# Gate and branch products interleaved in a hybrid encoder layer, with four of eight weight pairs as seven products in three gates

## The chip, the cores and the metric

The kernel runs on one core of one Trainium2 chip. The metric is device time in microseconds (us); of several runs of a kernel the median is given. TensorE (PE) multiplies, VectorE (DVE) and ScalarE (ACT) prepare operands and take results out of PSUM, GpSimd (POOL) does a few small things, and SyncE (SP) issues the weight loads.

## What is computed

One encoder layer on 256 tokens of 2048 features. The part around the change is the gated merge of two attention branches:

```python
h = rms_norm(x, norm_mix_pre[l])
proj = jnp.einsum('bsd,dc->bsc', h, w_in[l])
qa, ka, va, qn, kn, vn, gates = jnp.split(proj, split_at, axis=-1)
...
g_a, g_b = jnp.split(jax.nn.sigmoid(gates), N_BRANCHES, axis=-1)
mixed = (g_a * jnp.einsum('bsc,cd->bsd', oa, w_branch_a[l])
         + g_b * jnp.einsum('bsc,cd->bsd', on, w_branch_b[l]))
y = jnp.einsum('bsd,de->bse', mixed, w_out[l])
```

`oa` and `on` (256 x 1024) come from the two attentions. Behind `y` stand a residual, a norm and an MLP (2048 to 8192, squared ReLU, back to 2048) with another norm and residual.

## The kernel before, in words

All products are made in float32 precision from two-part operands: each operand is split into a rounded high part and the rest (`h` and `l` in the tile names), and a product takes three matmuls (high x high, high x low, low x high). A matmul of the wide products has a 128 x 128 stationary piece of the activations and 512 columns of weights.

The two gates and the two branch products are made in two halves of 1024 output columns (`h` = 0 and 1 in the code). Each is a wide group: the weights come in pairs, a pair being 256 rows x 1024 columns, loaded by one DMA of 1 MB. A gate has eight pairs (2048 rows), a branch product four (1024 rows). A group's results stand in PSUM banks named 1, 2, 3 and 7, one for each quarter of 128 tokens x 512 columns; other groups use the same four PSUM buffers in turn. There are two ways to multiply a pair:

- the plain way (`eight`, line 755): 4 quarters x 2 row blocks x 3 matmuls = 24 matmuls. ACT rounds the raw pair to its high part (line 675), DVE subtracts for the low part (line 677).
- seven products of sums (`seven`, line 743), a Winograd form of the 2 x 2 block product: 7 x 3 = 21 matmuls, into banks 1, 2, 3 and also 0, 4, 5 and 6. It needs sums of the weight blocks, so DVE makes three additions (lines 681 to 683), ACT rounds raw blocks (line 680) and sums (line 693), and DVE subtracts for their low parts (lines 684 and 694). It also needs sums of the activations, made once per pair in `h_sums` (line 824) while the first gate runs. Once the last such pair of a group is multiplied, `combine` (line 761) copies bank 0 (ACT, line 767) and makes four additions on DVE (lines 768 to 771), and so puts banks 0, 4, 5 and 6 into the result tiles in SBUF.

At the end of a group each quarter is taken out of its bank. A gate's quarter is added to the result tile if there were seven-product pairs (DVE, line 884) and goes through a sigmoid (ACT, line 885). A branch's quarter is multiplied with the gate (DVE, line 917), and for branch b added to that of branch a (line 919).

The order of the work is that of the code, refined by a scheduler that places every engine's instructions by a modelled timeline. The groups stand in the order ga, gb, ba, bb for each half; the list of weight requests (line 846 on) must have the same order. `Weights.next` keeps three pairs in hand: there are three buffers each for the raw, high and low weights, so a pair's high part waits until the pair three places earlier is multiplied, and its load until that pair is split. Five smaller buffers hold the split sums, of which a seven-product pair takes four. In the very first gate all eight pairs are plain; in the other three the list `MIXED` (line 841) says in which places stand the three seven-product pairs: pairs 0, 3 and 6, in places 1, 3 and 5 of places 0 to 7. While ba of the second half runs, the transposes of the first half's merged result (`mixed_T`, mT in the names) are put between its products. `y` follows bb of the second half.

Of the kernel before, what the change touches and what calls it, by code (L numbers as in the profile page):

```python
# [32 lines left out]
QA, KA, VA, QN, KN, VN, GA, GB = 0, 1024, 2048, 3072, 4096, 5120, 6144, 8192  # L33
# [17 lines left out]
def encoder_layer(ctx: ExitStack, tc: tile.TileContext, a, out):  # L51
# [13 lines left out]
    def page(shape, dt, name):  # L65
        return pages.tile(shape, dt, tag="pg", name=name)
# [4 lines left out]
    def t2k(name, dt=F32):  # L71
        return tmp.tile([P, 2, T], dt, tag="t2k", name=name, bufs=7)
# [128 lines left out]
    def advance(n):  # L201

        if chores:
            with tc.issue_after(last_load[0]):
                chores.pop(0)()
        for _ in range(n):
            if pending:
                g = pending.pop(0)
                if next(g, None):
                    pending.append(g)  # L210
# [507 lines left out]
    def columns(src, i, c):  # L718
        return src[i * T : (i + 1) * T, c : c + 1024].rearrange("(k p) c -> p k c", p=P)
# [53 lines left out]
    def wide_group(name, kinds, weights, stat7, stat8, mm_banks, z, piece, each=None, turn=None, after={}, in_order=False):  # L773

        any7 = any(s for _, s in kinds)
        pr = Products(name, mm_banks)
        pr.in_order = in_order
        for n, (i, seven) in enumerate(kinds):  # L780
            w = weights.next(after)
            if each:
                each(n)
            if seven:
                final = not any(s for _, s in kinds[n + 1 :])
                pr.seven(partial(stat7, i), w, final)
                if final:
                    pr.combine(z)
                continue
            end = n == len(kinds) - 1  # L790
            if turn and n < 2:
                ahead = [*ahead, (i, w)] if n else [(i, w)]
                for t in range(2) if n else ():
                    for ii, ww in ahead:
                        for which in (2 * t, 2 * t + 1):
                            pr.eight(partial(stat8, ii), ww, which, False)
                    if not t:
                        turn()
                continue
            for which in range(4):  # L800
                pr.eight(partial(stat8, i), w, which, end)
                if end:
                    b, t, half = PLAIN[which]
                    piece(t, half, pr.ps[b], any7)

    def sums_of(p1, p2, name):

        a11, a21, a12, a22 = p1[:, :P], p1[:, P:], p2[:, :P], p2[:, P:]
        s = page([P, 4, P], F32, f"{name}s")
        nc.vector.tensor_sub(s[:, 0], a21, a22)  # L810
        nc.vector.tensor_sub(s[:, 1], a11, a21)
        nc.vector.tensor_sub(s[:, 2], s[:, 0], a11)
        nc.vector.tensor_add(s[:, 3], a12, s[:, 2])
        parts_ = page([P, 2, 4, P], F32R, name)
        nc.scalar.copy(parts_[:, 0], s)
        nc.vector.tensor_sub(parts_[:, 1], s, parts_[:, 0].bitcast(F32))
        return parts_
# [5 lines left out]
    def h_sums(i):  # L823
        f = t2k(f"hf{i}")
        for k in range(2):
            d = hT[i][:, k].bitcast(F32)
            nc.vector.tensor_add(f[:, k], d[:, :T], d[:, T:])
        hsum[i] = sums_of(f[:, 0], f[:, 1], f"hs{i}")
# [9 lines left out]
        d = oT[o, i * 2 + k]  # L838
        return d[:, t * P : (t + 1) * P], d[:, T + t * P : T + (t + 1) * P]

    MIXED = [(1, 0), (0, 1), (2, 0), (3, 1), (4, 0), (6, 1), (5, 0), (7, 0)]
    ALL8 = [(i, 0) for i in range(8)]
    mT = []
    mixed = []
# [1 line left out]
    for h in range(2):  # L846
        for nm, src, c, kinds in (
            ("ga", w_in, GA, MIXED if h else ALL8),
            ("gb", w_in, GB, MIXED),
            ("ba", a["w_branch_a"], 0, ALL8[:4]),  # L850
            ("bb", a["w_branch_b"], 0, ALL8[:4]),
        ):
            for i, seven in kinds:
                gw.ask(columns(src, i, c + h * 1024), f"{nm}{h}_{i}", seven)
    gw.stop = 8

    def mixed_T(h, n):

        mh, ml = page([P, 4, T], F32R, f"mh{h}{n}"), page([P, 4, T], F32R, f"ml{h}{n}")
        for b in range(2):  # L860
            pt = bank(f"mT{h}{n}{b}")
            for j in range(2):
                for t in range(2):
                    c = (n * 4 + b * 2 + j) * P
                    nc.tensor.transpose(
                        pt[:, j * T + t * P : j * T + (t + 1) * P],
                        mixed[h][t].rearrange("p a b -> p (a b)")[:, c : c + P],
                        ident,
                    )
            at = slice(b * 2, b * 2 + 2)  # L870
            src = pt.rearrange("p (j q) -> p j q", j=2)
            nc.scalar.copy(mh[:, at], src)
            nc.vector.tensor_sub(ml[:, at], src, mh[:, at].bitcast(F32))
        mT.append((mh, ml))

    for h in range(2):
        gate = []
        for br, gc in (("a", GA), ("b", GB)):
            z = [page([P, 2, 512], F32, f"g{br}{h}{t}") for t in range(2)]

            def gate_piece(t, half, ps, summed, z=z):
                zt = z[t][:, half]
                if summed:
                    nc.vector.tensor_add(zt, zt, ps)
                nc.scalar.activation(
                    zt, zt if summed else ps, AF.Sigmoid, scale=rx[:, t : t + 1]
                )

            first_one = h == 0 and br == "a"

            def each(n):
                advance(2)
                if n >= 4 and n < 7:
                    h_sums((0, 3, 6)[n - 4])

            wide_group(
                f"g{br}{h}",
                ALL8 if first_one else MIXED,
                gw,
                hstat7,  # L900
                hstat8,
                (1, 2, 3, 7),
                z,
                gate_piece,
                each=each if first_one else None,
            )
            if first_one:
                advance(99)
                temps.close()
                mid = ctx.enter_context(tc.tile_pool(name="mid", bufs=5, reuse_waits="tile"))  # L910
                gw.stop = None
            gate.append(z)
        for br, src, o, z in (("a", a["w_branch_a"], "a", gate[0]), ("b", a["w_branch_b"], "n", gate[1])):

            def br_piece(t, half, ps, summed, z=z, br=br, gate=gate):
                zt = z[t][:, half]
                nc.vector.tensor_mul(zt, zt, ps)
                if br == "b":
                    nc.vector.tensor_add(gate[0][t][:, half], gate[0][t][:, half], zt)

            wide_group(
                f"b{br}{h}",
                ALL8[:4],
                gw,
                None,
                partial(ostat8, o),
                (1, 2, 3, 7),
                None,
                br_piece,
                each=(lambda n: mixed_T(0, n // 2) if n in (0, 2) else None) if h and br == "a" else None,  # L930
            )
        mixed.append(gate[0])
# [239 lines left out]
    for g in range(DFF // 1024):  # L1172
        z = Late(lambda g=g: [page([P, 2, 512], F32, f"u{g}{t}") for t in range(2)])
# [256 lines left out]
```

## Time and profile before

| | us |
|---|---|
| three runs | 1342.76, 1343.35, 1343.53 |
| median | 1343.35 |
| span of the profiled execution, first to last instruction | 1342.7 |
| PE busy in it | 1331.8 |
| DVE busy in it | 1060.9 |
| ACT busy in it | 727.8 |

The profiled execution is given by its span only; the three runs lie 0.06 to 0.83 us above that span. The profile's busy time of PE counts a matmul until its modelled end, so consecutive matmuls overlap in it: a single matmul of 512 columns shows as 0.39 us, and the next one begins earlier than that. For how long PE works on something, the spacing of the starts is read, as the chain of waits gives it.

### The profile page before, as it was taken

The numbers are of one execution on the slowest core, as the hardware profiler recorded it, in microseconds if no ns is written. First come the engines' busy times: TensorE is split into PE (matmuls) and PEld (weight loads), VectorE is DVE, ScalarE is ACT, GpSimd is POOL, SyncE is SP. The second block draws the span as 40 slices with busy tenths as digits, with TensorE's granted clock in tenths as the row PEclk, the third lists the DMA queues.
The fourth block names the chain that finished last, engine by engine and source line by source line (L and its number), as shares of the span: only waits on it lengthen the run. The fifth ranks groups of instructions, "written<-read, shape, count | busy, mean of one in ns | idle before, by whom it ended". The sixth has DMA issues, their size and how long they took to land.

```text
span 1342.7 us, 16224 instructions
## 1 busy us (share of the span) xinstructions
PE 1331.8 (99%) x6315; PEld 1116.9 (83%) x6315; DVE 1060.9 (79%) x1224; ACT 727.8 (54%) x857; POOL 38.5 (3%) x71
## 2 busy tenths in 40 slices
PE   9999999999999999999999999999999999999997
PEld 8888888888888888888888888888888888888885
DVE  7968866677857886655778999999888888898886
ACT  6655554545644454344476665666655555555542
POOL 0000000000000000000100000000000000000000
PEclk9999999999999999999999999999999999999999
DMA  9874755564556655586657677877797998798995
GB/s 347 264 216 164 203 162 183 179 190 157 188 188 208 215 202 184 181 291 193 220 188 265 239 246 277 289 244 246 251 360 289 400 374 318 273 367 335 353 354 202
DMA packets 116028, 335.85 MB, mean 250 GB/s; under 512 B 16752, under 2 KB 17008, under 8 KB 115952
## 3 DMA queue, kind: packets, MB, share of 16 engines
q1 hardware_dynamic: 96560, 266.13, 58.2%
q10 hardware_dynamic: 12672, 43.00, 8.5%
q0 software_dynamic: 6720, 25.69, 4.9%
q8 instruction: 49, 0.80, 0.2%
q14 instruction: 27, 0.22, 0.0%
HBM read 307.01 MB, written 29.61 MB: 251 GB/s over the span
## 4 chain that ended last, share of the span: by engine, by line
PE 98%; DVE 1%; DMA 0%; ACT 0%; DVEq 0%; issue 0%; POOLq 0%; POOL 0%; ACTq 0%
PE u L740 25%; PE p L740 24%; PE ga L740 6%; PE gb L740 6%; PE ba L740 3%; PE bb L740 3%; PE qa_p L221 2%; PE ka_p L221 2%; PE qn_p L221 2%; PE kn_p L221 2%; PE y_p L266 2%; PE y_p L265 2%; PE y_p L264 2%; PE qa_p L223 1%; PE qn_p L223 1%; PE ka_p L223 1%
## 5 line engine op out<-in xcount | busy, mean ns | idle before, releaser
L145 DVE TENSOR_TENSOR y_l<-y_w,y_h 128x1024 fp32r<-128x1024 f32 x32 | 37.9, 1222 | 30.9 <-ACT y_h L137 30.9
L137 ACT CAST y_h<-y_w 128x1024 fp32r<-128x1024 f32 x32 | 32.0, 1051 | 40.9 <-PE y_p L266 32.5
L264 PE MATMUL y_p<-y_h,mh 128*128 128x512 f32 x128 | 50.1, 391 | 0.0
L265 PE MATMUL y_p<-y_l,mh 128*128 128x512 f32 x128 | 49.9, 390 | 0.0
L266 PE MATMUL y_p<-y_h,ml 128*128 128x512 f32 x128 | 49.8, 390 | 0.0
L221 PE MATMUL qn_p<-hT,qn_h 128*128 128x512 f32 x128 | 45.8, 399 | 0.0
L221 PE MATMUL qa_p<-hT,qa_h 128*128 128x512 f32 x128 | 45.1, 413 | 0.5 <-DVE hT L305 0.5
L221 PE MATMUL kn_p<-hT,kn_h 128*128 128x512 f32 x128 | 45.3, 397 | 0.0
L221 PE MATMUL ka_p<-hT,ka_h 128*128 128x512 f32 x128 | 45.1, 398 | 0.0
L740 PE MATMUL u<-u_2h,h2T 128*128 128x512 f32 x128 | 44.0, 396 | 0.0
L740 PE MATMUL u<-u_1h,h2T 128*128 128x512 f32 x128 | 43.4, 390 | 0.0
L740 PE MATMUL u<-u_4h,h2T 128*128 128x512 f32 x128 | 43.2, 391 | 0.0
L740 PE MATMUL u<-u_7h,h2T 128*128 128x512 f32 x128 | 41.0, 389 | 0.0
L740 PE MATMUL u<-u_6h,h2T 128*128 128x512 f32 x128 | 41.0, 389 | 0.0
L223 PE MATMUL qn_p<-hT,qn_l 128*128 128x256 f32 x128 | 35.9, 281 | 0.0
L223 PE MATMUL kn_p<-hT,kn_l 128*128 128x256 f32 x128 | 35.7, 280 | 0.0
L223 PE MATMUL ka_p<-hT,ka_l 128*128 128x256 f32 x128 | 35.2, 282 | 0.0
L223 PE MATMUL qa_p<-hT,qa_l 128*128 128x256 f32 x128 | 32.8, 285 | 0.0
L221 PEld LDWEIGHTS qa_p<-hT,qa_h 128*128 128x128 f32 x128 | 24.5, 197 | 5.5 <-ACT qa_h L143 0.8
L221 PEld LDWEIGHTS qn_p<-hT,qn_h 128*128 128x128 f32 x128 | 24.0, 188 | 5.2
L221 PEld LDWEIGHTS kn_p<-hT,kn_h 128*128 128x128 f32 x128 | 23.9, 188 | 5.2
L221 PEld LDWEIGHTS ka_p<-hT,ka_h 128*128 128x128 f32 x128 | 23.9, 188 | 5.2
(1431 smaller groups left out, 4406.8 us busy)
## 6 DMA issues: line engine op xcount, KB each, us to landing
y_w<-in_w_out SPq DMA_DIRECT2D x16, 1024.0 KB, 5.3
bh<-keeph ACTq DMA_DIRECT2D x30, 512.0 KB, 9.6
bl<-keepl ACTq DMA_DIRECT2D x30, 512.0 KB, 11.0
keeph<-ah POOLq DMA_DIRECT2D x18, 512.0 KB, 3.6
keepl<-al POOLq DMA_DIRECT2D x18, 512.0 KB, 7.8
va_w<-in_w_in SPq DMA_DIRECT2D x8, 1024.0 KB, 5.3
qn_w<-in_w_in SPq DMA_DIRECT2D x8, 1024.0 KB, 5.1
kn_w<-in_w_in SPq DMA_DIRECT2D x8, 1024.0 KB, 5.2
```

Of the source, the lines that this page charges most:

```text
L137: nc.scalar.copy(hi[part], src)
L145: sub = nc.vector.tensor_sub(lo[part], src, hi[part].bitcast(F32)).ins
L221: nc.tensor.matmul(ps[b], hi[:, k % 4, cs], mv, start=(k == 0), stop=False)
L223: nc.tensor.matmul(ps[b][:, :T], lo[:, k % 4, cs], mv[:, :T], start=False, stop=(k == nk - 1))
L264: nc.tensor.matmul(ps[t], sh, hi[:, k % 4], start=(k == 0), stop=False)
L265: nc.tensor.matmul(ps[t], sh, lo[:, k % 4], start=False, stop=False)
L266: nc.tensor.matmul(ps[t], sl, hi[:, k % 4], start=False, stop=(k == nk - 1))
L740: ins = nc.tensor.matmul(self.ps[i], st, mv[:, blk], start=i not in self.begun, stop=last and n == 2).ins
```

## The change

In each half the branch product now follows its own gate: ga, ba, gb, bb. The weight requests follow the same order. `MIXED` has four seven-product pairs instead of three: pairs 0, 2, 4 and 6, in places 0, 2, 4 and 6 (the first, third, fifth and seventh), and the activation sums are made for those four pairs. The very first gate keeps eight plain pairs.

```diff
-    MIXED = [(1, 0), (0, 1), (2, 0), (3, 1), (4, 0), (6, 1), (5, 0), (7, 0)]
+    SUMMED = (0, 2, 4, 6)
+    MIXED = [(0, 1), (1, 0), (2, 1), (3, 0), (4, 1), (5, 0), (6, 1), (7, 0)]
...
             ("ga", w_in, GA, MIXED if h else ALL8),
+            ("ba", a["w_branch_a"], 0, ALL8[:4]),
             ("gb", w_in, GB, MIXED),
-            ("ba", a["w_branch_a"], 0, ALL8[:4]),
             ("bb", a["w_branch_b"], 0, ALL8[:4]),
...
-        for br, gc in (("a", GA), ("b", GB)):
+        for br, gc, src, o in (("a", GA, a["w_branch_a"], "a"), ("b", GB, a["w_branch_b"], "n")):
...
-                if n >= 4 and n < 7:
-                    h_sums((0, 3, 6)[n - 4])
+                if n >= 4:
+                    h_sums(SUMMED[n - 4])
...
-        for br, src, o, z in (("a", a["w_branch_a"], "a", gate[0]), ("b", a["w_branch_b"], "n", gate[1])):
```

Two places show what moves. In the rows a result bank is written as gate or branch, half, bank (gb11 is gate b, half 1, bank 1; the same letters with a small bank number are the result tiles), and a weight tile as group, half, pair and part (gb1_4h is the high part of pair 4; eh0 and el0 are the parts of its sums). A number behind the last underscore counts tiles.

On PE, pair 4 of gate b in the second half. Before, its first rows, all into the plain banks:

```order
L740 MATMUL gb11_4204<-gb1_4h_4278,hT4_129 128x512
L740 MATMUL gb11_4204<-gb1_4l_4279,hT4_129 128x512
L740 MATMUL gb11_4204<-gb1_4h_4278,hT4_129 128x512 x2
L740 MATMUL gb11_4204<-gb1_4l_4279,hT4_129 128x512
L740 MATMUL gb11_4204<-gb1_4h_4278,hT4_129 128x512
L740 MATMUL gb12_4211<-gb1_4h_4278,hT4_129 128x512
L740 MATMUL gb12_4211<-gb1_4l_4279,hT4_129 128x512
L740 MATMUL gb12_4211<-gb1_4h_4278,hT4_129 128x512 x2
```

In the changed program the same pair, from its tenth matmul to its last:

```order
L740 MATMUL gb14_4420<-gb1_4eh0_4478,hs4_3266 128x512
L740 MATMUL gb14_4420<-gb1_4el0_4479,hs4_3266 128x512
L740 MATMUL gb14_4420<-gb1_4eh0_4478,hs4_3266 128x512
L740 MATMUL gb16_4424<-gb1_4eh0_4478,hs4_3266 128x512
L740 MATMUL gb16_4424<-gb1_4el0_4479,hs4_3266 128x512
L740 MATMUL gb16_4424<-gb1_4eh0_4478,hs4_3266 128x512
L740 MATMUL gb15_4428<-gb1_4eh1_4482,hs4_3266 128x512
L740 MATMUL gb15_4428<-gb1_4el1_4483,hs4_3266 128x512
L740 MATMUL gb15_4428<-gb1_4eh1_4482,hs4_3266 128x512
L740 MATMUL gb13_4432<-gb1_4eh1_4482,hT4_129 128x512
L740 MATMUL gb13_4432<-gb1_4el1_4483,hT4_129 128x512
L740 MATMUL gb13_4432<-gb1_4eh1_4482,hT4_129 128x512
```

Pair 4 has become seven products of three matmuls, with the sums hs4 as stationary operand. Over the whole program the order holds 6,304 matmuls and transposes before and 6,295 now; behind the last product of bb, PE's order is the same in both.

On DVE, the end of the same gate. Before, from the last weight subtraction of the gate to the third of the next group (ba):

```order
L677 TENSOR_TENSOR gb1_7l_4379<-gb1_7r_4376,gb1_7h_4378 128x2048
L768 TENSOR_TENSOR gb10_4196<-gb10_4196,gb15_4269 128x512
L677 TENSOR_TENSOR ba1_0l_4411<-ba1_0r_4408,ba1_0h_4410 128x2048
L769 TENSOR_TENSOR gb11_4197<-gb10_4196,gb16_4265 128x512
L770 TENSOR_TENSOR gb10_4196<-gb14_4261,gb10_4196 128x512
L771 TENSOR_TENSOR gb11_4197<-gb14_4261,gb11_4197 128x512
L884 TENSOR_TENSOR gb10_4196<-gb10_4196,gb11_4204 128x512
L677 TENSOR_TENSOR ba1_1l_4441<-ba1_1r_4438,ba1_1h_4440 128x2048
L884 TENSOR_TENSOR gb10_4196<-gb10_4196,gb12_4211 128x512
L884 TENSOR_TENSOR gb11_4197<-gb11_4197,gb13_4218 128x512
L884 TENSOR_TENSOR gb11_4197<-gb11_4197,gb17_4225 128x512
L677 TENSOR_TENSOR ba1_2l_4479<-ba1_2r_4476,ba1_2h_4478 128x2048
```

In the changed program (line 884 is now 885, and the next group is bb):

```order
L677 TENSOR_TENSOR gb1_7l_4580<-gb1_7r_4577,gb1_7h_4579 128x2048
L694 TENSOR_TENSOR gb1_6el1_4553<-gb1_6t1_4542,gb1_6eh1_4552 128x1024
L677 TENSOR_TENSOR bb1_0l_4610<-bb1_0r_4607,bb1_0h_4609 128x2048
L768 TENSOR_TENSOR gb10_4387<-gb10_4387,gb15_4428 128x512
L677 TENSOR_TENSOR bb1_1l_4642<-bb1_1r_4639,bb1_1h_4641 128x2048
L769 TENSOR_TENSOR gb11_4388<-gb10_4387,gb16_4424 128x512
L885 TENSOR_TENSOR gb10_4387<-gb10_4387,gb11_4412 128x512
L770 TENSOR_TENSOR gb10_4387<-gb14_4420,gb10_4387 128x512
L771 TENSOR_TENSOR gb11_4388<-gb14_4420,gb11_4388 128x512
L885 TENSOR_TENSOR gb10_4387<-gb10_4387,gb12_4408 128x512
L885 TENSOR_TENSOR gb11_4388<-gb11_4388,gb13_4432 128x512
L885 TENSOR_TENSOR gb11_4388<-gb11_4388,gb17_4460 128x512
```

The last seven-product pair now stands in place 6, with one plain pair behind it instead of two. So the four additions of `combine` stand among the four that empty the gate's banks, and two weight subtractions of the next group stand ahead of the first of these.

## The prediction

> **What bounds the kernel now.** I read the page first: the busy times, the clock, and the chain that ended last.
>
> ```profile
> span 1342.7 us, 16224 instructions
> ...
> PE 1331.8 (99%) x6315; PEld 1116.9 (83%) x6315; DVE 1060.9 (79%) x1224; ACT 727.8 (54%) x857; POOL 38.5 (3%) x71
> ...
> PEclk9999999999999999999999999999999999999999
> ...
> PE 98%; DVE 1%; DMA 0%; ACT 0%; DVEq 0%; issue 0%; POOLq 0%; POOL 0%; ACTq 0%
> ```
>
> PE is on 98% of the chain, at full clock in every slice. A busy PE alone would prove little, since ends of matmuls are modelled; so I asked for PE's own waits.
>
> ```profile
> PE idle L171 <- POOL ones L163: 1.0, 1, 1.0
> PE qa_p L221 <- DVE hT L305: 0.5, 1, 0.5
> ```
>
> That is the whole list: two waits, both before the first product. From there to the tail PE never waits for an operand or a bank. So a matmul taken out shortens the span by its spacing, and nothing else can shorten it; and whatever makes PE wait lengthens it in full. The spacing is read in the chain in order of time (start, length, what), here the groups from gate b of the first half to ba of the second:
>
> ```profile
> 348.98 41.48 PE gb L740 x183
> 390.46 21.76 PE ba L740 x96
> 412.22 21.76 PE bb L740 x96
> 433.98 41.48 PE ga L740 x183
> 475.46 41.48 PE gb L740 x183
> 516.94 0.87 PE mT L865 x8
> 517.82 10.90 PE ba L740 x48
> ```
>
> Each group begins where the last one ends. A gate has 183 matmuls, which is 5 plain pairs of 24 and 3 of 21, in 41.48 us: 0.2267 us each. A branch has 96 in 21.76: the same 0.2267. So a plain pair is 5.44 us of PE and a seven-product pair 4.76.
>
> **The change part by part.** *Matmuls.* In each of three gates a plain pair becomes a seven-product pair: 3 x 3 = 9 matmuls fewer, 9 x 0.2267 = 2.04 us less. The two orders of PE differ by these 9. [...]
>
> *What the added pairs cost DVE and ACT.* The rows of DVE by shape, from gate b of the second half (busy, mean ns):
>
> ```profile
> L694 DVE TENSOR_TENSOR gb_6el<-gb_6t,gb_6eh 128x1024 fp32r<-128x1024 f32 x2 | 2.4, 1224 | 0.0
> L677 DVE TENSOR_TENSOR gb_5l<-gb_5r,gb_5h 128x2048 fp32r<-128x2048 f32 x1 | 2.3, 2284 | 0.0
> ...
> L684 DVE TENSOR_TENSOR gb_6l<-gb_6r,gb_6h 128x1536 fp32r<-128x1536 f32 x1 | 1.8, 1759 | 0.7 <-ACT gb_6h L680 0.7
> ...
> L681 DVE TENSOR_TENSOR gb_6t<-gb_6r 128x1024 f32<-128x1024 f32 x1 | 1.2, 1226 | 0.0
> ...
> L683 DVE TENSOR_TENSOR gb_6t<-gb_6t,gb_6r 128x512 f32<-128x512 f32 x1 | 0.7, 686 | 0.0
> L682 DVE TENSOR_TENSOR gb_6t<-gb_6t,gb_6r 128x512 f32<-128x512 f32 x1 | 0.7, 685 | 0.0
> ```
>
> A seven-product pair takes 1.23 + 0.69 + 0.69 + 1.76 + 2 x 1.22 = 6.81 us, a plain one 2.28: 4.53 us more in each of three gates. [...] Is there room? The windows of ba in the first half and of the two gates of the second (PE, PEld, DVE, ACT):
>
> ```profile
> 390.50:412.20 21.70, 21.70 (x97) 17.97 (x96) 11.59 (x9) 8.93 (x7) 0.00 (x0) 1.00 0.58 194
> 434.00:475.50 41.50, 41.50 (x184) 34.35 (x184) 36.19 (x34) 22.17 (x17) 0.00 (x0) 1.00 0.60 203
> 475.50:517.00 41.50, 41.50 (x186) 34.33 (x184) 32.45 (x30) 21.07 (x17) 0.00 (x0) 1.00 0.61 203
> ```
>
> With 4.53 more, DVE would have 40.7 or 37.0 us to do in a gate that lasts 41.48 - 0.68 = 40.8. Gate a of the second half is the brimful one, since the multiplications and additions of the branch before it end in its window. I counted it anew for the new order: pairs 2, 4 and 6 at 6.81, pairs 3, 5 and 7 and the next group's first two at 2.28, `combine`, the gate's four adds and the branch's eight operations at 0.68 come to 20.4 + 11.4 + 10.9 = 42.7 us of durations. In a row of DVE's work the next operation starts 0.08 before the last one's recorded end (2.29 long, 2.21 to the next start, in the rows of the gate's end below), so these 39 operations take 3.1 us less: 39.6 of 40.8. It fits, with 1.2 us over. The other two gates stand behind a branch a, which has four such operations, not eight, and behind every gate now comes a branch, where DVE works 11.59 of 21.7 us. The first pair of a gate, now a seven-product one, is prepared in the branch's last places. ACT, at 22.17 of 41.5, takes about 2 us more and has the room. So I put these costs at nothing, under the cover of PE's work; what they cost if the cover is thin is the lead of a pair over its use. For the third seven-product pair of gate b:
>
> ```profile
> L684 DVE TENSOR_TENSOR gb_6l<-gb_6r,gb_6h x1: 1759/1759/1759, 494.1 to 494.1; 128x1536 fp32r<-128x1536 f32 x1
> L740 PEld LDWEIGHTS gb<-gb_6l,hs x1: 188/188/188, 501.1 to 501.1; 128*128 128x128 f32 x1
> ```
>
> DVE is done at 495.9, PE takes it up at 501.1: 5.2 us ahead, after three such pairs in places 1, 3 and 5. If the whole 4.53 us came off this lead, 0.7 would be left.
>
> *The end of a gate.* Here the cover gets thinner: after the last seven-product pair stands one plain pair, not two, so 5.44 us less of PE's work hides `combine`. The next group's first matmul into bank 1 waits until the gate's bank 1 has been added. The DVE rows of before at that place:
>
> ```profile
> 503.32 2.29 DVE L677 TENSOR_TENSOR gb_7l<-gb_7r,gb_7h 128x2048 fp32r<-128x2048 f32 x1 [4.16 <-ACT gb_7h L675]
> 505.53 0.68 DVE L768 TENSOR_TENSOR gb<-gb,gb 128x512 f32<-128x512 f32 x1
> 506.13 2.28 DVE L677 TENSOR_TENSOR ba_0l<-ba_0r,ba_0h 128x2048 fp32r<-128x2048 f32 x1
> 508.33 0.68 DVE L769 TENSOR_TENSOR gb<-gb,gb 128x512 f32<-128x512 f32 x1
> ...
> 512.89 0.69 DVE L884 TENSOR_TENSOR gb<-gb,gb 128x512 f32<-128x512 f32 x1 [2.56 <-PE gb L740]
> 513.50 2.29 DVE L677 TENSOR_TENSOR ba_1l<-ba_1r,ba_1h 128x2048 fp32r<-128x2048 f32 x1
> ```
>
> There bank 1 was added by 513.6, and the gate ended at 516.9: 3.3 us to spare, and the add had itself waited 2.56 us for PE. Now the sum for the new order, from t = 0 at PE's first product of pair 6. The buffer for the next group's first high part comes free about then. Its rounding on ACT takes as long as this one:
>
> ```profile
> 503.86 1.92 ACT L675 CAST ba_0h<-ba_0r 128x2048 fp32r<-128x2048 f32 x1
> ```
>
> so about 2.1. Then DVE: bb_0l to 4.3 (2.2 from start to start); L768, which needs the 18th product of the pair, at 18 x 0.2267 + 0.16 = 4.24, so to 4.9 (0.60 from start to start); bb_1l to 7.1; L769 to 7.7; the add of bank 1 to 8.4. The gate ends at 45 x 0.2267 = 10.2. Margin 1.8 us. Bank 2's add follows L770 and L771 and ends at 10.2, and is needed 12 products into the next group, at 12.9. Nothing waits, if DVE is not more than 1.8 us late.
>
> *The first gate's end.* Its results now go to ba at once. ACT had there the rounding of an activation sum, a table load and four sigmoids:
>
> ```profile
> 340.00 0.62 ACT L815 CAST hs<-hs6s 128x512 fp32r<-128x512 f32 x1
> ...
> 345.12 1.28 ACT L885 ACT_TABLE_LOAD   x1
> 346.41 1.93 ACT L885 ACTIVATE ga<-ga,rx 128x512 f32<-128x512 f32 x3
> ```
>
> Bank 1 was free at 347.1, 1.9 us before 348.98. The fourth activation sum puts one more such rounding, 0.6 us, ahead of it; 1.3 are left. The first reader of the sums is gate b, now 21.76 us later.
>
> *What is moved.* The 16 transposes in ba of the second half are the same 16. The loads are the same 24 pairs a half, in the new order, on SP's queue; gpost, x and w_out follow as before. Behind bb PE's order is unchanged; DVE and ACT swap a few neighbours in the down products, by at most one subtraction of 2.28 us, where the lead is:
>
> ```profile
> L740 PE MATMUL p<-d0100el,bh x4: 389/389/389, 1130.1 to 1132.1; 128*128 128x512 f32 x4
> L694 DVE TENSOR_TENSOR d0100el<-d0100t,d0100eh x2: 1218/1220/1221, 1124.3 to 1125.5; 128x1024 fp32r<-128x1024 f32 x2
> ```
>
> The second subtraction ends at 1126.7, and PE takes it up from 1130.1: 3.4 us. That is nothing either.
>
> **The sum.** 1342.70 - 2.04 = 1340.66 us for the span. The median of the runs lies 0.65 above the span, so 1343.35 - 2.04 = 1341.31 us, 0.15% faster. A measurement of this kernel can tell about 0.2%, 2.69 us, from no change; this is less.
>
> **The rivals.** *Part of the gain goes into waits.* The margins of 1.3 to 1.8 us are sums of steps that each wait for another engine. If DVE comes late by one more subtraction, 2.2 us, at each of three gate ends, PE waits 3 x 0.4 = 1.2 us, and the time is 1342.5. Against it: before, DVE had idle time there. Chance 0.15; the time then lies between 1341.5 and 1345.
>
> *DVE becomes the bound (slower).* The place is the end of a gate. If the whole 4.53 us per gate pile up there, as the window's 40.7 of 40.8 us would have it, the add of bank 1 comes 4.53 - 1.8 = 2.7 us late, and PE waits 3 x 2.7 = 8.2 us: 1341.3 + 8.2 = 1349.5. It turns slower than before once the wait is over 0.68 us per gate, that is DVE over 2.5 us late. Against it: the branch behind every gate, the 1.2 us that even the fullest gate has over, and the 5.2 us lead. Chance 0.06.
>
> *More comes back than nine matmuls.* With no wait of PE's to remove, only the scatter of runs (0.77 us from lowest to highest) can bring 1340.66, the bound for faster. Chance 0.10.
>
> That the change does not do what it says is ruled out by the two orders.
>
> **How the numbers follow.** The forecast, 2.04 us less with all else hidden, has 0.69; read within the scatter it is "no change". Faster by over 0.2% gets 0.10, from the scatter. Slower by over 0.2% (1346.0) gets 0.06, DVE's pile-up. Within 0.2% lie the forecast and the partial waits: 0.69 + 0.15 = 0.84. The range begins at 1341.3 - 0.8 = 1340.5, the scatter, and goes up to 1344.0, a wait of 0.9 us at each of three gate ends.
>
> **What would show it.** In the profile after: three gates of 180 matmuls in 40.80 us each; no wait of PE in the list besides the first two; the add of bank 1 (L885) done 1 to 2 us before the next group's first product. A wait of PE on L885 or L886, or on a low part (L677, L684, L694), would say which margin failed. The prediction is wrong if the spacing is no longer 0.2267, or if the span loses more than 2.04 us.

## The result, and the profile after

| | median, us | lowest to highest | runs |
|---|---|---|---|
| before | 1343.47 | 1342.76 to 1344.45 | 21 |
| after | 1341.61 | 1341.05 to 1342.25 | 21 |

The ratio is 0.9986, 95% interval 0.9980 to 0.9992: 1.86 us less, where 2.04 was forecast. That is less than 0.2%, so "within 0.2%" is what happened, 0.3 us above the forecast of 1341.3 and inside the range.

The page of the changed kernel has the same picture as before: PE busy for nearly the whole span.

```profile
span 1339.9 us, 16240 instructions
...
PE 1328.2 (99%) x6306; PEld 1112.9 (83%) x6306; DVE 1076.7 (80%) x1246; ACT 732.3 (55%) x864; POOL 38.5 (3%) x71
```

DVE has 22 instructions more and is busy for 15.8 us more. PE's own waits (line waited for, us in total, times, longest):

```profile
PE idle L171 <- POOL ones L163: 1.0, 1, 1.0
PE qa_p L221 <- DVE hT L305: 0.7, 2, 0.5
PE qa_p L223 <- DVE qa_l L145: 0.3, 1, 0.3
PE ka_p L221 <- DVE rope_s L291: 0.3, 1, 0.3
```

Two lines are new, but both belong to the projections at the start, over 300 us ahead of anything that the change touches. No gate and no branch is in the list. The chain of waits in order of time shows the groups (start, length, what):

```profile
348.20 21.76 PE ba L740 x96
369.96 40.80 PE gb L740 x180
...
432.97 40.35 PE ga L740 x178
...
496.93 40.80 PE gb L740 x180
537.73 21.76 PE bb L740 x96
559.49 0.23 PE y_p L264
```

A gate has 180 matmuls in 40.80 us (gate a of the second half shows 178, because two of its matmuls were drawn ahead among those of bb). The spacing is still 0.2267 us. From the end of the first gate, 348.20, to the first product of `y`, 559.49, pass 211.29 us. Before, gate b began at 348.98 and bb of the second half ended at 540.48 + 21.76 = 562.24: 213.26 us. The difference is 1.97 us, nine spacings less 0.07 that ba with its transposes takes longer.

The span fell by more, 2.8 us. The missing 0.8 us lies ahead of the first gate's end, which stands at 348.98 in the one profile and at 348.20 in the other. The two differ from PE's first real matmuls on; here the row of before and, in the second fence, the row of after (start, length, and what was waited for):

```profile
5.73 2.05 PE L221 MATMUL qa_p<-hT,qa_h 128*128 128x512 f32 x4 [0.53 <-DVE hT L305]
```

```profile
5.14 1.17 PE L221 MATMUL qa_p<-hT,qa_h 128*128 128x512 f32 x4 [0.51 <-DVE hT L305]
```

The same four matmuls took 2.05 and 1.17 us and end 1.5 us apart (7.78 against 6.31); by the first gate's end 0.8 us of that are left. What slowed them was not tried. In the eleven profiles of this case PE does the same 1,878 matmuls and transposes in the same order up to there, and the first gate ends anywhere from 347.29 to 348.98 us, in the four with the old order of groups from 347.39 to 348.98. So it is taken as scatter of the start, and not as a gain of the change.

### The profile page after: what moved, and what is told of

It reads as the page before. It is cut to its first block, busy times and chain, and to the rows that moved or that the text cites. A ratio compares the mean times of both kernels' runs of the same rounds, so it can differ in the third digit from the quotient of the medians.

```text
span 1339.9 us, 16240 instructions
## 1 busy us (share of the span) xinstructions
PE 1328.2 (99%) x6306; PEld 1112.9 (83%) x6306; DVE 1076.7 (80%) x1246; ACT 732.3 (55%) x864; POOL 38.5 (3%) x71
## 4 chain that ended last, share of the span: by engine, by line
PE 96%; DMA 1%; DVE 1%; ACT 0%; SPq 0%; issue 0%; DVEq 0%; POOLq 0%; POOL 0%; ACTq 0%
PE u L740 25%; PE p L740 24%; PE ga L740 6%; PE gb L740 6%; PE ba L740 3%; PE bb L740 3%; PE qn_p L221 2%; PE kn_p L221 2%; PE y_p L266 2%; PE y_p L265 2%; PE y_p L264 2%; PE ka_p L221 2%; PE qn_p L223 1%; PE kn_p L223 1%; PE qa_p L221 1%; PE vn_p L264 1%
## 5 line engine op out<-in xcount | busy, mean ns | idle before, releaser
L740 PEld LDWEIGHTS u<-u_1h,h2T 128*128 128x128 f32 x128 | 24.0, 188 | 5.0
```

Of the source, the lines that this page charges most:

```text
L740: ins = nc.tensor.matmul(self.ps[i], st, mv[:, blk], start=i not in self.begun, stop=last and n == 2).ins
```

## The experiments

The theory: a matmul taken out of the gates is worth its spacing, and DVE's larger share is hidden; the margin of that cover stands at the end of a gate, on the add of bank 1. The rivals: the new order of the groups has a part in the gain; the cover is larger, or stands elsewhere. All times are medians. In each experiment the loss of PE is read in the trace from the first gate's end to the first product of `y`, which leaves out the scatter of the start. (In the kernel as printed, `seven`, `eight` and `combine` begin at lines 746, 758 and 764, and `h_sums` at line 823.)

**The order alone.** Three seven-product pairs as before, in the new order:

```diff
-    SUMMED = (0, 2, 4, 6)
-    MIXED = [(0, 1), (1, 0), (2, 1), (3, 0), (4, 1), (5, 0), (6, 1), (7, 0)]
+    SUMMED = (0, 3, 6)
+    MIXED = [(1, 0), (0, 1), (2, 0), (3, 1), (4, 0), (6, 1), (5, 0), (7, 0)]
...
-                if n >= 4:
+                if n >= 4 and n < 7:
```

> The new order of groups (each branch behind its gate) with the three seven-product pairs of before, in places 1, 3 and 5: 6,304 matmuls and transposes, as before. Theory (the gain is the nine matmuls and nothing else): three gates of 183 matmuls in 41.48 us each, no wait of PE behind the first product, from the first gate's end to y's first product 213.3 us as before, and the time of before, 1343.5 us, to within 0.4. Rival (the order itself gives a part, by waits or by a closer sequence of groups): the stretch from the first gate's end to y is shorter than 213.0 and the time nearer to 1342.5 or below.

Measured: 1343.00 us beside 1343.23 for before, ratio 0.9999 (0.9990 to 1.0008). The chain of this kernel:

```profile
347.29 21.76 PE ba L740 x96
369.05 41.48 PE gb L740 x183
...
538.80 21.76 PE bb L740 x96
```

From 347.29 to 560.56 it is 213.27 us, as before (213.26). The order by itself moves nothing; the rival falls.

**No seven-product pair at all.** All eight pairs of every gate plain, in the new order (`MIXED` is the list of `ALL8`, `SUMMED` is empty, and no activation sum is made).

> All four gates with eight plain pairs, new order, no activation sums and no final additions: 6,295 + 36 matmuls. It measures the price of a matmul by the time itself, beyond the scatter of the runs. Theory (a matmul left out is worth its spacing of 0.2267 us): 36 x 0.2267 = 8.16 us over the changed kernel, 1349.8 us, gates of 192 matmuls in 43.53 us. [...] Rival (the DVE and ACT work that goes with the seven-product pairs delays something, so that they are worth less than their matmuls): under 7.5 us over, below 1349.1.

Measured: 1349.74 us, 8.13 over the changed kernel. The chain:

```profile
348.09 21.76 PE ba L740 x96
369.85 43.52 PE gb L740 x192
...
545.72 21.76 PE bb L740 x96
```

Here the question is only the size of a matmul, with 36 of them instead of nine, so that the scatter matters little. The time gives 8.13 / 36 = 0.226 us each; the gates give 43.52 / 192 = 0.2267; and from 348.09 to 545.72 + 21.76 = 567.48 it is 219.39 us, 8.10 more than in the changed kernel. So the rival, that the work on DVE and ACT takes something back, falls. The median of before moved by 0.24 us from one series of runs to the next, which over 36 matmuls leaves the price of one open by 0.007 us in the time alone; the spacing in the chain gives it directly.

**The four pairs alone.** Four seven-product pairs in the old order ga, gb, ba, bb (the lines for `SUMMED`, `MIXED` and `h_sums` of the change, nothing else of it).

> Four seven-product pairs in places 0, 2, 4 and 6 in the old order ga, gb, ba, bb: the nine matmuls are gone, but gate b follows gate a at once. Theory (DVE's margins are thin and the branch behind each gate is the cover): gate a's end and gate b's start collide on DVE; PE waits somewhat under 1 us at the start of gate b, for a high part of one of its first pairs, so of 2.04 us some 1.2 to 1.4 are left: about 1342.2 us. Rival 1 (the cover is not needed): no wait of PE, three gates in 40.80 us, 1341.5 us. Rival 2 (DVE becomes the bound when two seven-product gates follow each other): several microseconds of waits on DVE's results in gate b, over 1345 us.

Measured: 1341.24 us, ratio 0.9986 (0.9977 to 0.9995), the same ratio as the whole change. The chain of waits, and below it, from DVE's row of work, the add of bank 1 at the end of gate a of the second half:

```profile
347.39 40.80 PE gb L740 x180
...
431.71 40.80 PE ga L740 x180
472.51 40.83 PE gb L740 x180
...
536.94 21.76 PE bb L740 x96
```

```profile
471.36 0.68 DVE L885 TENSOR_TENSOR ga<-ga,ga 128x512 f32<-128x512 f32 x1
```

From 347.39 to 558.70 it is 211.31 us. No gate waits. My theory of this run, that gate b right behind gate a costs some 0.8 us, falls: on DVE the end of gate a and the start of gate b do run into each other, with work for gate b (lines 681, 682 and 684) between the adds of gate a, but PE loses nothing by it. The add ends at 472.04 and gate b begins at 472.51; these 0.5 us are not a margin, though, as the next experiment shows that gate b's first products do not wait for that add. So with four pairs the cover of the branch is not needed. What it is worth shows only when DVE gets more work.

**One subtraction more at the gate ends, in both orders.** DVE makes one low part of the next group twice, and the add of bank 1 stands behind that:

```diff
+    again = [None]
...
                 nc.vector.tensor_sub(l1, raw, h1.bitcast(F32))
+            if name in ("ba1_1", "bb0_1", "bb1_1"):
+                for _ in range(1):
+                    again[0] = nc.vector.tensor_sub(l1, raw, h1.bitcast(F32)).ins
...
-                    nc.vector.tensor_add(zt, zt, ps)
+                    with tc.issue_after(again[0]) if (t, half) == (0, 1) else nullcontext():
+                        nc.vector.tensor_add(zt, zt, ps)
```

In the old order the names are `ba0_1`, `gb1_1` and `ba1_1`. Line 885 becomes 891.

> The changed kernel with one more 2.2 us subtraction on DVE at each of the three gate ends (the low part of the next branch's second pair is made twice), and the add of bank 1 ordered behind it. Without it that add ends 1.9 us before the next group's first product in front of both bb, and 12 transposes (1.3 us) more lie ahead of ba. Theory (bank 1's add is what the next group waits for, and its margin is 1.9 us): PE waits 0.3 us on L891 at each bb and not at ba; a wait of 0.29 us cost 0.55 us of the sequence with five pairs, so 1.1 us over the changed kernel, about 1342.7. Rival (the margin is larger, or the add is not what is waited for): no wait, 1341.6.

> Four pairs in the old order ga, gb, ba, bb, with one more 2.2 us subtraction and the add of bank 1 behind it at the three gate ends. Without it that add ends 0.5 us before gate b of the second half and 1.5 us before ba of the first half; ahead of ba of the second half stand transposes. Theory (the branch behind each gate is cover that four pairs do not use up, but more DVE work does): waits of 1.7 us and 0.7 us, 0.25 more lost behind each, so 2.9 us over the four pairs in the old order (about 1344.1), against 1.1 in the new one. Rival (the order makes no difference to the cover): the same loss as in the new order, 1.1 us or none.

In the new order: 1342.81 us, 1.20 over the changed kernel. DVE at the end of gate b, second half, and PE at the same place:

```profile
535.64 2.29 DVE L682 TENSOR_TENSOR bb_1l<-bb_1r,bb_1h 128x2048 fp32r<-128x2048 f32 x1
537.84 0.68 DVE L891 TENSOR_TENSOR gb<-gb,gb 128x512 f32<-128x512 f32 x1
```

```profile
537.82 0.39 PE L745 MATMUL gb<-gb_7h,hT 128*128 128x512 f32 x1
538.67 0.47 PE L745 MATMUL bb<-bb_0h,onT 128*128 128x512 f32 x1 [0.46 <-DVE gb L891]
538.98 0.39 PE L745 MATMUL bb<-bb_0l,onT 128*128 128x512 f32 x1
```

PE waits for L891 at both bb and not at ba, as the theory said. Each costs 0.62 + 0.08 = 0.70 us of the sequence (0.85 and 0.31 from start to start instead of 0.2267), 1.4 together. From the first gate's end to `y` PE loses 1.5 us. In the old order: 1344.27 us, 3.03 over the four pairs alone (expected 2.9), and 3.0 us lost by PE in the same stretch. PE's waits in it:

```profile
PE ba L745 <- DVE gb L891: 0.7, 1, 0.7
...
PE gb L745 <- DVE ga L891: 0.5, 1, 0.5
PE gb L745 <- DVE gb_2el L699: 0.4, 1, 0.4
PE gb L745 <- ACT gb_2h L685: 0.3, 1, 0.3
```

At ba of the first half the theory is right: a wait of 0.7 us on the add of bank 1, 1.0 us lost with what follows. At gate b of the second half its 1.7 us on that add did not come. Gate b's first three matmuls began at 473.52 while the add of bank 1 ended only at 475.41, so they do not wait for it; PE lost 2.05 us there in three smaller waits, on the high part of pair 2, on a low part of its sums, and on the second of the gate's adds. That the total came out at the expected 2.9 is luck in this half.

The same edit costs 1.2 us by the medians (1.5 by the stretch) in the new order and 3.0 in the old; beside each other the two kernels differ by 1344.27 - 1342.81 = 1.5 us. Here the rival "the order makes no difference to the cover" falls.

**Two subtractions more.** The same in the new order with `range(2)`.

> As with one repeat, but two of them at each gate end; the add of bank 1 then also stands behind the other additions of the gate's end. Theory: at bb it ends at 14.0 us after the first product of the last seven-product pair where 10.2 are there, so a wait of about 3.9 us at each bb and of about 2.6 at ba, with 0.25 more lost behind each: 11 us over the changed kernel, about 1352.6. Rival (DVE makes up for it, since it has idle time in the gate): under 4 us over, below 1345.6.

Measured: 1355.71 us, 14.1 over the changed kernel instead of 11. The profile is of the longest of the four runs, 1357.86 us. The waits in the list are the ones expected, in their places: 7.7 us in two on L891 at bb, 2.0 at ba. What came on top stands behind them (PE at the end of gate b, first half):

```profile
410.01 0.39 PE L745 MATMUL gb<-gb_7h,hT 128*128 128x512 f32 x1
414.26 0.76 PE L745 MATMUL bb<-bb_0h,onT 128*128 128x512 f32 x1 [3.86 <-DVE gb L891]
414.82 0.63 PE L745 MATMUL bb<-bb_0l,onT 128*128 128x512 f32 x1
415.25 1.05 PE L745 MATMUL bb<-bb_0h,onT 128*128 128x512 f32 x2
416.10 0.63 PE L745 MATMUL bb<-bb_0l,onT 128*128 128x512 f32 x1
```

The starts are 0.43 us apart, not 0.23, up to 419.94. The windows of the same stretch (busy time of PE, PEld, DVE, ACT and POOL, then the granted clock, the share of TensorE's full clock that it was given):

```profile
405.00:411.00 6.00, 5.40 (x24) 4.13 (x22) 6.00 (x6) 0.56 (x1) 0.00 (x0) 1.00 0.52 175
411.00:414.20 3.20, 0.00 (x0) 0.00 (x0) 3.20 (x4) 1.38 (x2) 0.00 (x0) 0.87 0.00 0
414.20:420.00 5.80, 5.74 (x14) 4.51 (x15) 5.06 (x5) 2.51 (x4) 0.00 (x0) 0.50 0.70 199
```

The clock falls to 0.50 toward the end of the wait and stays there to the end of the window. In the profiled execution the three waits themselves cost 4.0 + 2.3 + 4.0 = 10.3 us of PE's sequence from start to start (2.3 at ba and not 2.6, as all 16 transposes stood ahead of it, not 12), and the slow matmuls behind them 2.9 + 1.8 + 1.7 = 6.4. From the first gate's end to `y` PE loses 16.5 us in all. So the theory's sum for the waits is about right, and the rest is a loss that it did not have.

**The same wait, with PE kept busy.** Sixteen matmuls into a spare bank fill the wait at both bb; nobody reads them.

```diff
+                if self.name in ("gb0", "gb1"):
+                    lasts[0] = ins
...
+            if name in ("bb0", "bb1") and n == 0:
+                spare = bank(f"spare{name}")
+                st = stat8(i, 0, 0)[0]
+                dead = lasts[0]
+                for _ in range(16):
+                    with tc.issue_after(dead):
+                        dead = nc.tensor.matmul(spare, st, w[0][:, 1], start=True, stop=True).ins
+                pr.after = dead
```

`lasts[0]` is the gate's last matmul, and `pr.after` puts the group's first product behind the sixteen.

> As two repeats at each gate end, but PE spends the wait at both bb on 16 matmuls whose results nobody reads (16 x 0.2267 = 3.6 of the 4.0 us between the gate's last matmul and the add of bank 1). Two repeats came to 1355.7 us and a span of 1356.1 instead of the expected 1352.6, and behind both waits of 3.9 us matmuls stood 0.43 us apart for some 3 to 6 us at a granted clock of 0.50. Theory (the idle time of PE itself takes the clock down): the first products of both bb stand at the same places behind the gates, but 0.2267 apart and at clock 1.00; of the 6.0 us lost behind the three waits the 4.3 at both bb go, the 1.7 at ba stay, so a span of 1351.8 and a time of 1351 to 1352.6. Rival (the slow matmuls come from what else runs then: loads, ACT and DVE at work behind the gate's end): they stay, and the time too, 1355 to 1357.

Measured: 1352.64 us (expected 1351 to 1352.6), span 1351.3 (expected 1351.8). PE at the end of gate b, first half, and the windows:

```profile
409.74 0.39 PE L746 MATMUL gb<-gb_7h,hT 128*128 128x512 f32 x1
409.96 3.79 PE L796 MATMUL sparebb<-bb_0h,onT 128*128 128x512 f32 x16
413.89 0.50 PE L746 MATMUL bb<-bb_0h,onT 128*128 128x512 f32 x1
414.23 0.40 PE L746 MATMUL bb<-bb_0l,onT 128*128 128x512 f32 x1
```

```profile
413.80:420.00 6.20, 6.11 (x27) 5.04 (x28) 5.55 (x7) 2.86 (x5) 0.00 (x0) 1.00 0.67 198
```

The first product of bb still comes 4.15 us after the gate's last (4.25 without the filling), with DVE and the loads at work as before, but the 6.2 us behind it hold 27 matmuls at clock 1.00, where the 5.8 us without the filling held 14 at 0.50. The wait of 2.0 us at ba was not filled, and the slow matmuls behind it stayed (1.75 us lost). So in these two runs the half clock at bb came with PE's own idle time of 3.9 us and went with it, and the rival falls.

**Five pairs.** A fifth seven-product pair, pair 5, in the three gates:

```diff
-    SUMMED = (0, 2, 4, 6)
+    SUMMED = (0, 2, 4, 5, 6)
-    MIXED = [(0, 1), (1, 0), (2, 1), (3, 0), (4, 1), (5, 0), (6, 1), (7, 0)]
+    MIXED = [(0, 1), (1, 0), (2, 1), (3, 0), (4, 1), (5, 1), (6, 1), (7, 0)]
...
-                if n >= 4:
-                    h_sums(SUMMED[n - 4])
+                if n >= 3:
+                    h_sums(SUMMED[n - 3])
```

> A fifth seven-product pair, pair 5 in place 5, in each of the three gates, new order: 6,286 matmuls and transposes. If DVE still had room, another 9 x 0.2267 = 2.04 us less than with four pairs: 1339.6 us. Theory (in the fullest gate DVE has only about 1 us over with four pairs, and a fifth adds 4.53): PE waits for DVE at the gates' ends, on the next group's bank 1, and on low parts, some 4 us in all, so about 1343.5 us; the waits stand in the list of PE. Rival (DVE's room is larger than counted, since the branches take up what is late): no waits, 1339.6 us.

> Five seven-product pairs in three gates, in the old order. In the new order the same pairs lost 4.4 us to waits and came to 1344.1. Theory (the branch is the cover): gates a and b of the second half stand one behind the other, DVE would have 39.3 + 36.3 + 2 x 4.5 = 84.7 us to do in their 80.2, and gate b of the first half 41.7 in 40.1, so PE loses these 6.1 us on top of some 2 us at the gates' ends: 1339.4 + 8 = 1347.5. Rival (the order does not matter): 1344.1 as in the new order, within 0.5.

In the new order: 1344.05 us (1343.49 to 1345.65), ratio 1.0010 (1.0001 to 1.0019) to before. PE's waits in it, behind the start:

```profile
PE bb L740 <- DVE bb_2l L677: 1.9, 1, 1.9
...
PE bb L740 <- DVE gb L885: 0.6, 2, 0.3
```

From the first gate's end to `y` it takes 213.67 us where another nine matmuls fewer should have made 209.25: 4.4 us are lost, as the theory had it, and on the engine and lines that it named. The fifth pair's gain of 2.04 us is paid twice over. The list of PE's waits adds up to only 2.8 of the 4.4, with a wait of 0.3 at the transposes. PE at one of the small ones:

```profile
409.02 0.39 PE L740 MATMUL gb<-gb_7h,hT 128*128 128x512 f32 x1
409.69 0.50 PE L740 MATMUL bb<-bb_0h,onT 128*128 128x512 f32 x1 [0.29 <-DVE gb L885]
410.03 0.39 PE L740 MATMUL bb<-bb_0l,onT 128*128 128x512 f32 x1
```

A wait of 0.29 us costs 0.67 - 0.23 = 0.44 before the waiting matmul and 0.34 - 0.23 = 0.11 behind it, 0.55 in all.

In the old order: 1345.54 us. The direction is the theory's, the size is not: PE loses 6.2 us there (215.47 from the first gate's end to `y`), against 4.4 in the new order, not the 8 that I had expected. I had counted all of DVE's overload as PE's wait; where part of it went was not tried.

## Why the prediction was right

- **Nine matmuls at 0.2267 us.** Right: 1.97 us in the chain, 1.86 in the medians. With 36 matmuls the time itself gives 0.226 each. No wait was taken away, the order alone gives nothing, so the nine matmuls are the whole gain.
- **The gate's end.** The sum had the add of bank 1 done 1.8 us ahead of the next group. DVE there, gate b of the second half:

```profile
529.55 2.29 DVE L677 TENSOR_TENSOR bb_0l<-bb_0r,bb_0h 128x2048 fp32r<-128x2048 f32 x1 [4.40 <-ACT bb_0h L675]
531.76 0.68 DVE L768 TENSOR_TENSOR gb<-gb,gb 128x512 f32<-128x512 f32 x1
532.36 2.28 DVE L677 TENSOR_TENSOR bb_1l<-bb_1r,bb_1h 128x2048 fp32r<-128x2048 f32 x1
534.56 0.68 DVE L769 TENSOR_TENSOR gb<-gb,gb 128x512 f32<-128x512 f32 x1
535.16 0.68 DVE L885 TENSOR_TENSOR gb<-gb,gb 128x512 f32<-128x512 f32 x1
```

The add of bank 1, in the last row, is done at 535.84, and bb begins at 537.73 in the chain: 1.9 us. The chain counts a matmul from the end of the one before it; the first matmul of bb itself starts at 537.56, which makes the margin 1.7. One added subtraction of 2.2 us made PE wait 0.46 us, which gives 1.7 as well; that this add is what PE waits for first at bb is shown by the same run.
- **The first gate's end.** 1.3 us were left by the sum. ACT in the changed kernel:

```profile
346.07 1.84 ACT L886 ACTIVATE ga<-ga,rx 128x512 f32<-128x512 f32 x3
```

The first of the three sigmoids is over by about 346.8 (a third of 1.84 behind the start, and some overlap), 1.4 us ahead of 348.20.
- **DVE's room in the fullest gate.** I counted 39.6 of 40.8 us for gate a of the second half. The window of it has less:

```profile
433.00:473.30 40.30, 40.30 (x180) 33.31 (x180) 36.78 (x36) 20.10 (x15) 0.00 (x0) 1.00 0.67 220
```

36 operations, not 39, and 36.8 us: the count was on the safe side by 2.8 us, since one of the operations (line 681 of pair 2) ran before the gate and two of the gate's own adds behind it. For the decision it made no difference.
- **The cover of the branch.** I gave "behind every gate now comes a branch" as a reason why DVE's work fits. At four pairs that reason was not needed: the old order holds too, without a wait in any gate. It begins to count when DVE has more to do, 1.5 us at one more subtraction (1344.27 against 1342.81) and 1.5 us at five pairs (1345.54 against 1344.05).
- **From the span to the median.** I took the span plus 0.65 us. That failed: the changed kernel's profiled execution took 1341.70 us at a span of 1339.9, 1.8 more, and the other kernels' runs lie about as far above their own spans. So the profiled execution of before was not a typical one: it took about 1342.7 + 1.8 = 1344.5, 1.1 above the median, and its first gate ended later than in any other profile here. The forecast escaped it, as it took the difference off the median.
- **The signs of being wrong.** By its letter one of them came: the span lost 2.8 us, more than 2.04, and the list has two lines of PE's waits more than the two foreseen. Both belong to the start of the program, where the profile of before was late. In the stretch from the first gate's end to `y` PE took 1.97 us less and waited nowhere. The sign should have been put on that stretch, not on the span of one execution.
- **"Whatever makes PE wait lengthens it in full."** That was too little. A listed wait of 0.46 us cost 0.70 of the sequence, and the waits of two added subtractions, 10.3 us of the sequence, drew slow matmuls behind them that cost 6.4 us more.
- **The rivals.** Neither the partial waits nor DVE as the bound came. Both are real mechanisms one pair further: with five pairs PE waits on the adds of bank 1 and on a low part, and the time is above before. Their prices can be held against the added subtractions. For 2.2 us at each gate's end the prediction had three waits of 0.4, 1.2 us; there were two, as transposes stand ahead of ba, at 0.70 each. For a pile-up of 4.53 us it had 8.2 us; two subtractions, 4.4 us, cost 14.1 in the median.

## What to carry to other kernels

Where one engine is on the whole chain and never waits, an instruction taken off it is worth its start-to-start spacing and no more (here 0.2267 us a matmul, and 0.226 by the time of 36); the rest of the work is to find which margin the other engine's added work uses up, and here two sums (DVE's row of work at the gate's end, and its total in the fullest window) were enough. A margin that holds is not a gain, and reordering that widens it shows no time until something uses it: the new order was worth nothing with four pairs, 1.5 us with one subtraction more. Beyond the margin the loss was steeper here than the lateness: a listed wait of 0.46 us cost 0.70, and behind three waits of 2.0 to 3.9 us slow matmuls cost 6.4 us more.

## What the runs showed of the hardware

- Two waits of PE cost more than the list of waits says: 0.55 us for 0.29 with five pairs, 0.70 for 0.46 with one repeat. The first matmul behind them is recorded as 0.50 and 0.47 us long, not 0.39, and the next starts 0.34 and 0.31 later, not 0.23.
- Behind long waits of PE, matmuls came slower. With two repeats the first wait at bb was 3.86 us long; behind it the granted clock was 0.50 and the starts stood 0.427 us apart, from 414.82 to 419.94. Behind the other two, one of 2.02 us right after 16 transposes and one of 3.86, the matmuls began 0.23 to 0.35 us apart, and stood 0.43 apart only from 1.6 us behind the wait on, for 3.0 us (485.27 to 488.25, 553.59 to 556.58); in the window from 486 to 488 the clock was 0.50. Filling the waits at both bb with matmuls that nobody reads saved 3.1 us in the median (1355.71 to 1352.64). The wait of 2.02 us at ba was not filled there, and behind it the starts were again 0.43 us apart, from 481.81 to 484.37.
- A wait of 1.89 us in the kernel with five pairs was followed by matmuls at a clock of 1.00. What decides whether, when and for how long the clock falls behind a wait was not shown.
- The four runs with two repeats lie between 1354.63 and 1357.86 us, and the runs with five pairs in two groups, 1343.49 to 1344.05 and 1345.31 to 1345.65. Slow matmuls behind a wait in only some of the runs would do that: the granted clock, as a mean over the run, is 0.993 in the longest with two repeats and 0.995 in the shortest, and 0.996 to 0.997 in the upper group with five pairs against 0.997 to 0.998 in the lower. The longer runs were not profiled in the case of five pairs, so it is not shown there.
- The start of the program scatters by 1.7 us: with the same work of PE, the first gate ended between 347.29 and 348.98 in eleven profiles.
